# Channel tiles in another order, the key weights' low parts on VectorE, and five small places beside 47 large ones

## The chip, the cores and the metric

The kernel runs on one core of a Trainium2 chip. Its time is the device time of one launch in microseconds (us), as a median of several runs. In the profile PE is TensorE, DVE is VectorE, ACT is ScalarE, POOL is GpSimd, and SP (SyncE) issues all DMAs. Another kernel of this size is told apart from it where the two differ by some 0.2%, that is 2.3 us.

## The reference

One layer of a streaming encoder for 1024 tokens of width 1024, in fp32, with three parts, each between two root-mean-square norms and added to the input:

```python
h = rms_norm(x, pre_mix_g[l])
z = h @ w_in[l] + b_in[l]                       # 1024 -> 1792
y_a = pool_mixer(z_a, ...)                      # trailing-window means, windows 2, 4, 8, 16
y_b = spatial_gating_mixer(z_b, ...)            # gelu, layer norm, 128-position mixing
y_c = conformer_conv_mixer(z_c, ...)            # a * sigmoid(g), causal conv of 31 taps, layer norm, silu
x = x + rms_norm(concat(y_a, y_b, y_c) @ w_out[l], post_mix_g[l])
h = rms_norm(x, pre_x_g[l]); m = rms_norm(mem, mem_g[l])
x = x + rms_norm(memory_cross_attention(h, m, wq[l], wk[l], wv[l], wo[l]), post_x_g[l])
h = rms_norm(x, pre_ff_g[l])
x = x + rms_norm(square(relu(h @ w_ff1[l])) @ w_ff2[l], post_ff_g[l])
```

The memory has 256 tokens, the attention 4 heads of 256, the last part 4096 hidden columns.

## The kernel before

**Arithmetic.** An fp32 factor is split into a high part of type fp32r and a low part (factor minus high part), and a product is three matmuls: high by high, low by high, high by low (`mm3`, L445). The high part is a cast on ACT; the low part is one subtraction on DVE or POOL, called "lo" below (`lo_of`, L438; tile names end in h and l). The large projections (output projection om, queries pq, attention output ox, both parts of the feed-forward part, FF1 and FF2) are done with seven half-size products in place of eight (`seven`, L991).

**Stages.** First x is normed and transposed (p0t, `norm_in`, L558). Then come the channel tiles of the convolution: for j = 0 to 2 (128 channels each) and the two halves hf of the tokens, PE makes zg and za (L602 on); ACT makes sg, the sigmoid of zg; DVE makes hc, the gated channels, and hs, a sum of neighbouring tokens. A convolution of 31 taps over one j needs hc[j] and hs[j] of both halves. It is 47 DVE instructions over rows of 512 (`conv_taps`, L644; accumulators cacca, caccb, caccc). While DVE works on the three j, PE goes on with the gating part (zb, sv, ybt), the pooling part (zaT, pya), the values of the memory (wvp) and the keys of the memory (wkp, from memory tiles mT). Then the convolution's result cs is transposed into token order (cnat), normed over channels (cst, cmv, then cr..e on DVE and cr..r on POOL, a reciprocal square root, then cn on DVE), transposed back (cback), gated on ACT (csg) and put into yq, which the output projection reads (`conv_norm`, L666). The keys are transposed as well (kt, from kn; kT). After that om begins.

**Weights of the first stages.** `row_unit` (L504) loads 128 rows of a weight as 128x1024, casts them on ACT and makes the lo either in one DVE instruction of 128x1024 or in two POOL instructions of 128x512, by the lists ZR, WK and WV (L519). WK are the keys' weights, tiles wk0 to wk7.

**Storage.** All large tiles in on-chip memory lie in NS = 50 places of 4 KB per partition with the tag "s" (`slot`, L113; `put`, L123 gives the recorded tile its place at the end). A tile of 512 floats, such as hs or sg, takes a whole place. The DMA that loads a tile waits until the place's former tile has been read for the last time.

**Order.** The class `Schedule` (L66) records every operation with its dependences, then puts them in order by a list schedule (`_order`, L249) with a cost for each operation (`_cost`, L204), a latency between engines and, for all engines but PE, a due time: that of the PE instruction it serves, or for those that serve none, the end plus SLACK (L82). `order` (L231) does this six times, feeding the order of PE back, and keeps the order with the shortest planned span. A DMA also depends on the PE operation that was recorded 150 before (LEAD). So a number in a cost or a changed number of places moves instructions of every engine, all over the program. On the chip each engine runs its own list in that order, and waits at an instruction whose input isn't there.

Of the kernel before, what the change touches and what calls it, by code (L numbers as in the profile page):

```python
# [20 lines left out]
NK = D // P  # L21
# [5 lines left out]
WINDOWS = (2, 4, 8, 16)  # L27
TAPS = 31
LEAD = 150
NS = 50  # L30


class _Op:
# [32 lines left out]
class Schedule:  # L66
# [12 lines left out]
           "pe": {"act": 197, "dve": 196, "pe": 0, "pool": 200, "sync": 100},  # L79
           "pool": {"act": 75, "dve": 60, "pe": 309, "pool": 102, "sync": 100},  # L80
           "sync": {"act": 2100, "dve": 2100, "pe": 2100, "pool": 2100, "sync": 2100}}
    SLACK = 50000.0  # L82
    PASSES = 6
    BYDUE = ("act", "dve", "pool", "sync")
    TABLE = {AF.Sigmoid: "sigmoid", AF.Gelu_apprx_tanh: "gelu", AF.Exp: "exp"}
# [25 lines left out]
        self.pool, self.places, self.form = pool, n, form  # L111

    def slot(self, name, shape, dt):  # L113
        self._add("s:" + name, "s", self.places)
        self.tiles["s:" + name].update(shape=[128] + list(shape), dt=dt, ap=None)
        n = int(np.prod(shape))
        t = self.form[:, :n]
        if len(shape) > 1:
            d = "abc"[:len(shape)]
            t = t.rearrange(f"p ({' '.join(d)}) -> p {' '.join(d)}", **dict(zip(d, shape)))  # L120
        return _Slot("s:" + name, t if dt == F32 else t.bitcast(dt))

    def put(self, a):  # L123
        if not isinstance(a, _Slot):
            return a
        r = self.tiles[a.name]
        if r["ap"] is None:
            r["ap"] = self.pool.tile(r["shape"], r["dt"], tag=f"s{r['at']}", name=a.name[2:])
        return a.place(r["ap"])


# [71 lines left out]
    @staticmethod  # L203
    def _cost(eng, method, args, kw, ins):  # L204
        n = 1
        for d in args[0].shape[1:]:
            n *= d
        if method == "dma_start":
            return max(450.0, n * args[0].shape[0] * 4 / 240.0)
        size = lambda a: int(np.prod(a.shape[1:]))  # L210
        if eng == "pe":
            passes = 4 if method == "matmul" and args[1].dtype == F32 else 1
            return max(109.0, 13.4 + passes * n * 0.4167)
        wide = [a for a in ins if size(a) > 1]
        ptrs = len(ins) - len(wide) if n > 1 else 0
        if eng == "act":
            c = 51.0 + 0.833 * n + (0.0 if ins[0].space == bass.MemoryType.PSUM else 42.0)
            return c + 93.0 * min(ptrs, 1) + (93.0 if "accum_out" in kw else 0.0)
        if eng == "pool":
            if method == "tensor_tensor":  # L220
                return 520.0 if n < 17 else 60 + 2.4 * n
            return 60 + 1.0 * n
        n = max([n] + [size(a) for a in wide])
        psum = any(a.space == bass.MemoryType.PSUM for a in ins + [args[0]])
        if not psum and len(wide) == 1 and method in ("tensor_scalar", "tensor_scalar_mul",
                                                      "tensor_copy"):
            return 69 + 0.52 * n + 61.0 * ptrs
        return 69 + 1.042 * n + 61.0 * ptrs
# [174 lines left out]
def block_kernel(ctx: ExitStack, tc: tile.TileContext, x, mem, pre_mix_g, w_in, b_in, pool_w,  # L403
# [5 lines left out]
    act, dve, pool, pe, sync = sc.act, sc.dve, sc.pool, sc.pe, sc.sync  # L409
# [106 lines left out]
            return hi, lo  # L516
        return go

    ZR, WK, WV = [pool] * NK, [pool] * NK, [dve] * NK  # L519
    units, made = {}, {}  # L520
    for j in range(3):
        units[f"zc{j}"] = col_unit(f"zc{j}", [(w_in, 1024 + j * P), (w_in, 1408 + j * P)], j == 0)
# [76 lines left out]

    hc = [slot(f"hc{j}", [2, H]) for j in range(3)]  # L600
    hs = [slot(f"hs{j}", [H]) for j in range(3)]
    for j, hf in ((0, 0), (1, 0), (0, 1), (1, 1), (2, 0), (2, 1)):  # L602
        w = W(f"zc{j}")
        pa, pg = bank(f"za{j}{hf}"), bank(f"zg{j}{hf}")
        if (j, hf) == (0, 0):
            for q in range(2):
                if q:
                    norm_in(0, [2, 3])
                prod_t(pg, w, 128, 256, h1[hf], q * 256, q * 256 + 256)
                prod_t(pa, w, 0, 128, h1[hf], q * 256, q * 256 + 256)  # L610
            W("zc1")
            norm_in(1, [0, 1, 2, 3])
            (g_x, g_ff, g_mem, bA, bC, pscale, cb, clg, clb, sgb) = columns("vec", [
                (pre_x_g, 8), (pre_ff_g, 8), (mem_g, 8), (b_in[:, 0:256], 2), (b_in[:, 1024:1792], 6),
                (pool_scale, 2), (conv_b, 3), (conv_ln_g, 3), (conv_ln_b, 3), (sg_b[0], 4)])
            cw = columns("taps", [(conv_w[0].rearrange("k (j p) -> (k j) p", p=P), 93)])[0].rearrange(
                "p (k j) -> p k j", j=3)
        else:
            prod_t(pg, w, 128, 256, h1[hf])
            prod_t(pa, w, 0, 128, h1[hf])  # L620
        sg = slot(f"sg{j}{hf}", [H])
        act.activation(sg, pg, AF.Sigmoid, bias=bC[:, 3 + j:4 + j])
        c = slice(hf * 256, hf * 256 + 256)
        dve.scalar_tensor_tensor(hc[j][:, :, c], pa.rearrange("p (n t) -> p t n", t=2),
                                 bC[:, j:j + 1], sg.rearrange("p (n t) -> p t n", t=2),
                                 ALU.add, ALU.mult)
        dve.tensor_tensor(hs[j][:, c], hc[j][:, 0, c], hc[j][:, 1, c], ALU.add)
# [131 lines left out]
    for hf in range(2):  # L759
        for m in range(2):  # L760
            zaT[hf][m] = slot(f"zaT{hf}{m}", [H + 16])
        for pr in range(2):
# [3 lines left out]
            for i in range(2):  # L766
                b = pr * 2 + i
                p0, p1 = bank(f"zb0{hf}{b}"), bank(f"zb1{hf}{b}")
                for k in range(NK):
                    a = h1[hf][k]  # L770
# [15 lines left out]
                r = rstd_of(f"vr{hf}{b}", mv[:, 1:2], 1)  # L786
# [32 lines left out]
    for t in range(2):  # L819
# [4 lines left out]
        r = rstd_of(f"memr{t}", ms, 1)  # L824
# [475 lines left out]
    for u in range(2, HF // 256):  # L1300
        w, h, rest = ff1(u)
# [29 lines left out]
    for ch in range(2):  # L1331
# [17 lines left out]
        for i, g, first in ((1, 0, True), (2, 1, True), (6, 0, False), (5, 1, True), (7, 0, False),  # L1349
                            (3, 1, False), (4, 0, False)):  # L1350
            ops = []
            for e in range(4):
# [13 lines left out]
                a = slot(f"ha{ch}{i}{e}", [2, H])  # L1366
# [66 lines left out]
```

## Time and profile before

| | |
|---|---|
| time, median of 3 runs | 1169.54 us (1169.51 to 1169.66) |
| the profiled execution's own time | 1169.37 us |
| its span, first to last instruction | 1167.7 us |
| PE busy | 1142.2 us, 98% |
| DVE busy | 917.0 us, 79% |
| ACT busy | 570.9 us, 49% |
| POOL busy | 168.2 us, 14% |
| mean granted TensorE clock | 0.995 |
| DMA | 163.11 MB, 140 GB/s in the mean |

The span leaves 1.7 us of the execution outside. An engine's busy time is summed over its instructions; the granted clock is the part of full speed that the chip gave TensorE. The waits of an engine are listed with the instruction that ended them, and the timeline gives each instruction's start and duration.

### The profile page before, as it was taken

The numbers are of one execution on the slowest core, as the hardware profiler recorded it, in microseconds if no ns is written. First come the engines' busy times: TensorE is split into PE (matmuls) and PEld (weight loads), VectorE is DVE, ScalarE is ACT, GpSimd is POOL, SyncE is SP. The second block draws the span as 40 slices with busy tenths as digits, with TensorE's granted clock in tenths as the row PEclk, the third lists the DMA queues.
The fourth block names the chain that finished last, engine by engine and source line by source line (L and its number), as shares of the span: only waits on it lengthen the run. The fifth ranks groups of instructions, "written<-read, shape, count | busy, mean of one in ns | idle before, by whom it ended". The sixth has DMA issues, their size and how long they took to land.

```text
span 1167.7 us, 14569 instructions
## 1 busy us (share of the span) xinstructions
PE 1142.2 (98%) x5319; PEld 948.6 (81%) x5319; DVE 917.0 (79%) x1278; ACT 570.9 (49%) x998; POOL 168.2 (14%) x194
## 2 busy tenths in 40 slices
PE   7999999799999999999999999999999999999997
PEld 6788877688887898888888888888888888888885
DVE  5499999898988769988999777567679744487736
ACT  6332145666984368749843343334446433435321
POOL 4360229301347000013000000000000000000001
PEclk9999999899999999999999999999999999999999
DMA  7400025114761222236045535443775444443443
GB/s 263 146 30 1 1 89 207 47 62 150 256 253 55 90 72 91 73 119 225 17 136 210 186 137 184 158 146 116 241 263 189 162 163 155 153 160 116 174 144 145
DMA packets 87078, 163.11 MB, mean 140 GB/s; under 512 B 6474, under 2 KB 29918, under 8 KB 87006
## 3 DMA queue, kind: packets, MB, share of 16 engines
q1 hardware_dynamic: 87006, 162.17, 39.8%
q8 instruction: 42, 0.69, 0.2%
q14 instruction: 30, 0.25, 0.1%
HBM read 116.01 MB, written 46.14 MB: 139 GB/s over the span
## 4 chain that ended last, share of the span: by engine, by line
PE 87%; DVE 7%; ACT 4%; issue 1%; POOL 0%; DMA 0%; POOLq 0%; DVEq 0%; ACTq 0%
PE g L162 25%; PE fx L162 13%; PE fz L162 7%; PE om L162 7%; PE pq L162 6%; PE ox L162 5%; PE zb L162 4%; PE fy L162 3%; PE zg L162 3%; PE za L162 3%; PE sc L162 2%; PE o L162 2%; PE wvp L162 2%; PE wkp L162 2%; DVE caccc L162 1%; ACT oxh L162 1%
## 5 line engine op out<-in xcount | busy, mean ns | idle before, releaser
L162 POOL TENSOR_TENSOR fr0r<-fr0e,half 128x1 f32<-128x1 f32 x1 | 0.9, 863 | 581.9 <-DVE fr0e L162 581.9
L162 ACT COPY c<-fx 128x512 f32<-128x512 f32 x48 | 29.0, 603 | 87.8 <-PE fx L162 84.6
L162 DVE TENSOR_TENSOR acc<-acc,g 128x512 f32<-128x512 f32 x40 | 26.9, 684 | 46.1 <-PE g L162 46.1
L162 DVE TENSOR_TENSOR c<-c,fz 128x512 f32<-128x512 f32 x32 | 22.0, 687 | 16.5 <-ACT c L162 16.5
L162 DVE SCALAR_TENSOR_TENSOR c<-c 128x512 f32<-128x512 f32 x48 | 33.3, 693 | 0.7
L162 DVE SCALAR_TENSOR_TENSOR caccc<-hs,cws,caccc 128x511 f32<-128x511 f32 (+14 forms) x45 | 33.5, 744 | 0.2
L162 DVE SCALAR_TENSOR_TENSOR cacca<-hc,taps,cacca 128x511 f32<-128x511 f32 (+14 forms) x45 | 32.2, 746 | 0.0
L162 ACT ACTIVATE junk<-acc 128x512 f32<-128x512 f32 x16 | 10.2, 635 | 44.7 <-DVE acc L162 42.7
L162 DVE TENSOR_TENSOR w1o<-w1a,w1o 128x512 fp32r<-128x512 f32 x32 | 21.6, 689 | 12.6 <-ACT w1o L162 12.6
L162 DVE SCALAR_TENSOR_TENSOR caccb<-hc,taps,caccb 128x511 f32<-128x511 f32 (+13 forms) x42 | 30.5, 745 | 0.0
L162 PE MATMUL sc<-kv,q 128*128 128x256 f32 x192 | 27.5, 288 | 0.0
L162 ACT CAST w1o<-w1a 128x512 fp32r<-128x512 f32 x32 | 19.6, 640 | 14.7 <-DVE sb L162 6.2
L162 PEld LDWEIGHTS sc<-kv,q 128*128 128x128 f32 x192 | 24.9, 190 | 0.7
L162 DVE TENSOR_TENSOR sa<-c 128x512 f32<-128x512 f32 x16 | 11.1, 695 | 18.0 <-ACT c L162 16.5
L162 ACT ACTIVATE c<-fx 128x512 f32<-128x512 f32 x16 | 9.6, 598 | 31.6 <-PE fx L162 31.6
L162 PE MATMUL o<-pT,kv 128*128 128x512 f32 x96 | 24.4, 393 | 0.0
L162 ACT CAST w1o<-w1c 128x512 fp32r<-128x512 f32 x32 | 19.5, 624 | 6.9 <-PE fx L162 4.1
L162 PE MATMUL fx<-h3a10h,w1o 128*128 128x512 f32 x64 | 22.7, 392 | 0.0
L162 DVE TENSOR_TENSOR w1o<-w1c,w1o 128x512 fp32r<-128x512 f32 x32 | 21.6, 689 | 1.2 <-ACT w1o L162 1.2
L162 PE MATMUL fx<-h3a60h,w1o 128*128 128x512 f32 x64 | 22.5, 389 | 0.0
L162 PE MATMUL fx<-h3a11h,w1o 128*128 128x512 f32 x64 | 22.3, 389 | 0.0
L162 PE MATMUL fx<-h3a70h,w1o 128*128 128x512 f32 x64 | 22.3, 389 | 0.0
(1656 smaller groups left out, 4116.8 us busy)
## 6 DMA issues: line engine op xcount, KB each, us to landing
ha<-scr_hid SPq DMA_DIRECT2D x56, 512.0 KB
scr_hid<-c SPq DMA_DIRECT2D x48, 256.0 KB
scr_hid<-sa SPq DMA_DIRECT2D x32, 256.0 KB
scr_hid<-sb SPq DMA_DIRECT2D x32, 256.0 KB
x<-in_x_dram SPq DMA_DIRECT2D x8, 512.0 KB
omwb<-in_w_out_dram SPq DMA_DIRECT2D x8, 512.0 KB
omx<-in_x_dram SPq DMA_DIRECT2D x8, 512.0 KB
scr_x<-omx SPq DMA_DIRECT2D x8, 512.0 KB
```

Source lines behind the costliest of these rows:

```text
L162: op.fn = lambda: f(*[put(a) for a in args], **{k: put(v) for k, v in kw.items()})
```

## The change

The 50 places of 4 KB become 47, and five places of 2 KB with the tag "h" come beside them. Tiles with names that begin with hs or sg and that have at most 528 elements per partition go to the small places: hs0 to hs2, the six sg of the channel tiles, and sgr, the raw mixing matrix. SLACK is 20000 in place of 50000, and the schedule's rate for a DMA 260 in place of 240. The list WK names DVE in place of POOL: eight lo of 128x1024 on DVE in place of sixteen of 128x512 on POOL. The channel tiles come in the order (j, hf) = (0,0), (0,1), (1,0), (1,1), (2,0), (2,1); before, (1,0) stood second.

```diff
--- before.py
+++ after.py
@@ -27,7 +27,10 @@
 WINDOWS = (2, 4, 8, 16)
 TAPS = 31
 LEAD = 150
-NS = 50
+NS = 47
+NH2 = 5
+SMALL = 528
+HALF = ("hs", "sg")
 
 
 class _Op:
@@ -79,7 +82,7 @@
            "pe": {"act": 197, "dve": 196, "pe": 0, "pool": 200, "sync": 100},
            "pool": {"act": 75, "dve": 60, "pe": 309, "pool": 102, "sync": 100},
            "sync": {"act": 2100, "dve": 2100, "pe": 2100, "pool": 2100, "sync": 2100}}
-    SLACK = 50000.0
+    SLACK = 20000.0
     PASSES = 6
     BYDUE = ("act", "dve", "pool", "sync")
     TABLE = {AF.Sigmoid: "sigmoid", AF.Gelu_apprx_tanh: "gelu", AF.Exp: "exp"}
@@ -111,7 +114,10 @@
         self.pool, self.places, self.form = pool, n, form
 
     def slot(self, name, shape, dt):
-        self._add("s:" + name, "s", self.places)
+        if int(np.prod(shape)) <= SMALL and name.startswith(HALF):
+            self._add("s:" + name, "h", NH2)
+        else:
+            self._add("s:" + name, "s", self.places)
         self.tiles["s:" + name].update(shape=[128] + list(shape), dt=dt, ap=None)
         n = int(np.prod(shape))
         t = self.form[:, :n]
@@ -125,7 +131,7 @@
             return a
         r = self.tiles[a.name]
         if r["ap"] is None:
-            r["ap"] = self.pool.tile(r["shape"], r["dt"], tag=f"s{r['at']}", name=a.name[2:])
+            r["ap"] = self.pool.tile(r["shape"], r["dt"], tag=f"{r['tag']}{r['at']}", name=a.name[2:])
         return a.place(r["ap"])
 
 
@@ -206,7 +212,7 @@
         for d in args[0].shape[1:]:
             n *= d
         if method == "dma_start":
-            return max(450.0, n * args[0].shape[0] * 4 / 240.0)
+            return max(450.0, n * args[0].shape[0] * 4 / 260.0)
         size = lambda a: int(np.prod(a.shape[1:]))
         if eng == "pe":
             passes = 4 if method == "matmul" and args[1].dtype == F32 else 1
@@ -516,7 +522,7 @@
             return hi, lo
         return go
 
-    ZR, WK, WV = [pool] * NK, [pool] * NK, [dve] * NK
+    ZR, WK, WV = [pool] * NK, [dve] * NK, [dve] * NK
     units, made = {}, {}
     for j in range(3):
         units[f"zc{j}"] = col_unit(f"zc{j}", [(w_in, 1024 + j * P), (w_in, 1408 + j * P)], j == 0)
@@ -599,7 +605,7 @@
 
     hc = [slot(f"hc{j}", [2, H]) for j in range(3)]
     hs = [slot(f"hs{j}", [H]) for j in range(3)]
-    for j, hf in ((0, 0), (1, 0), (0, 1), (1, 1), (2, 0), (2, 1)):
+    for j, hf in ((0, 0), (0, 1), (1, 0), (1, 1), (2, 0), (2, 1)):
         w = W(f"zc{j}")
         pa, pg = bank(f"za{j}{hf}"), bank(f"zg{j}{hf}")
         if (j, hf) == (0, 0):
```

Four views of how the instructions move follow. On DVE, behind the constants of the convolution, before: the digits behind za and sg are j and hf.

```order
L162 SCALAR_TENSOR_TENSOR hc0_1079<-za00_90,vec_118,sg00_1072 128x2x256
L162 SCALAR_TENSOR_TENSOR hc1_1087<-za10_122,vec_118,sg10_1077 128x2x256
L162 TENSOR_TENSOR hs0_1092<-hc0_1079 128x256
L162 TENSOR_TENSOR hs1_1096<-hc1_1087 128x256
L162 SCALAR_TENSOR_TENSOR hc0_1079<-za01_124,vec_118,sg01_1117 128x2x256
L162 TENSOR_TENSOR hs0_1092<-hc0_1079 128x256
L162 TENSOR_SCALAR cacca0_234<-hc0_1079,taps_120 128x512
L162 TENSOR_SCALAR caccb0_235<-hc0_1079,taps_120 128x512
```

After, at the same place:

```order
L168 SCALAR_TENSOR_TENSOR hc0_1070<-za00_90,vec_118,sg00_1061 128x2x256
L168 TENSOR_TENSOR hs0_1078<-hc0_1070 128x256
L168 SCALAR_TENSOR_TENSOR hc0_1070<-za01_122,vec_118,sg01_1065 128x2x256
L168 TENSOR_TENSOR hs0_1078<-hc0_1070 128x256
L168 TENSOR_SCALAR cacca0_234<-hc0_1070,taps_120 128x512
L168 TENSOR_SCALAR caccb0_235<-hc0_1070,taps_120 128x512
```

The third channel tile was gated ahead of the first tap before (cacca is the first accumulator); now the taps begin behind the second. All six tiles are still made, and the other four stand among the taps.

On POOL, in the stretch in which the lo of the keys' weights were made, before (zw are the window sums of the pooling part, cr00r to cr13r the convolution norm's reciprocal roots for eight token blocks):

```order
L162 TENSOR_TENSOR wk4l<-wk4r,wk4h 128x512
L162 TENSOR_TENSOR zw_2314<-zw_2291 128x521
L162 TENSOR_TENSOR wk5l<-wk5r,wk5h 128x512
L162 TENSOR_TENSOR zw_2351<-zw_2314 128x513
L162 TENSOR_TENSOR wk5l<-wk5r,wk5h 128x512
L162 TENSOR_TENSOR wk6l<-wk6r,wk6h 128x512 x2
L162 TENSOR_TENSOR wk7l<-wk7r,wk7h 128x512 x2
L162 TENSOR_TENSOR cr00r<-cr00e,half 128x1
```

After, from the first zw of the second token half:

```order
L168 TENSOR_TENSOR zw_2207<-zaT_1774 128x527
L168 TENSOR_TENSOR zw_2225<-zw_2207 128x525
L168 TENSOR_TENSOR zw_2241<-zaT_1793 128x527
L168 TENSOR_TENSOR vr13r<-vr13e,half 128x1
L168 TENSOR_TENSOR cr00r<-cr00e,half 128x1
L168 TENSOR_TENSOR zw_2279<-zw_2241 128x525
L168 TENSOR_TENSOR zw_2293<-zw_2279 128x521
L168 TENSOR_TENSOR zw_2311<-zw_2293 128x513
L168 TENSOR_TENSOR cr01r<-cr01e,half 128x1
```

The wk rows are gone from POOL, and cr00r stands ahead of the last three zw.

On DVE, behind the last tap of the third j, after (zz and vv belong to the gating part, oma10l and oma11l are the low parts of om's second product):

```order
L168 TENSOR_TENSOR wk0l<-wk0r,wk0h 128x1024
L168 BN_STATS vst_194<-zz_2091 128x6
L168 TENSOR_TENSOR wk1l<-wk1r,wk1h 128x1024
L168 BN_AGGR vmv_195<-vst_194 128x2
L168 TENSOR_TENSOR oma10l<-yq_1931,oma10h 128x1024
L168 TENSOR_SCALAR vr12e<-vmv_195 128x1
L168 SCALAR_TENSOR_TENSOR zz_2091<-zz_2091,vmv_195,sgn 128x384
L168 TENSOR_TENSOR oma11l<-yq_1649,oma11h 128x1024
L168 SCALAR_TENSOR_TENSOR vv_2154<-zz_2091,vr12r,sgn 128x384
L168 TENSOR_TENSOR wk2l<-wk2r,wk2h 128x1024
L168 TENSOR_TENSOR wk3l<-wk3r,wk3h 128x1024
L168 TENSOR_TENSOR wk4l<-wk4r,wk4h 128x1024
```

The five rows that write wk0l to wk4l are new on DVE; wk5l to wk7l follow some 35 rows later. The row oma11l, which came behind the last omww11l before, stands ahead of them.

On PE, at the end of the keys' products, before:

```order
L162 MATMUL wkp_229<-wk7l,mT_2212 128x512
L162 MATMUL wkp_229<-wk7h,mT_2238 128x512
L162 MATMUL cback_256<-ident,cn_2471 128x128
L162 MATMUL cback_255<-ident,cn_2490 128x128 x2
L162 MATMUL cback_256<-ident,cn_2490 128x128
L162 MATMUL kt_230<-ident,kn_2442 128x128
L162 MATMUL kt_230<-ident,kn_2463 128x128
L162 MATMUL kt_230<-ident,kn_2442 128x128
L162 MATMUL kt_230<-ident,kn_2463 128x128
L162 MATMUL cnat_286<-ident,cs_1549 128x128
L162 MATMUL cnat_286<-ident,cs_1692 128x128
L162 MATMUL cnat_286<-ident,cs_1703 128x128
```

After:

```order
L168 MATMUL wkp_229<-wk7h,mT_2231 128x512
L168 MATMUL wkp_229<-wk7l,mT_2231 128x512
L168 MATMUL wkp_229<-wk7h,mT_2246 128x512
L168 MATMUL kt_230<-ident,kn_2529 128x128
L168 MATMUL kt_231<-ident,kn_2529 128x128
L168 MATMUL kt_232<-ident,kn_2529 128x128
L168 MATMUL kt_233<-ident,kn_2529 128x128
L168 MATMUL kt_230<-ident,kn_2546 128x128
L168 MATMUL kt_230<-ident,kn_2529 128x128
L168 MATMUL kt_230<-ident,kn_2546 128x128
L168 MATMUL kt_231<-ident,kn_2546 128x128
L168 MATMUL kt_231<-ident,kn_2529 128x128
```

Before, the transposes cback, kt and cnat alternate here, each for another block or key column. After, all but the last two groups of cback and all cnat stand further ahead, singly between the wkp products, and kt and om follow on the keys' products.

## Rows read from the trace of the kernel before

**Rows 1.** The head of the page: the span of the execution and, in part 1, the busy time of each engine, its share of the span and its count of instructions.

```profile
span 1167.7 us, 14569 instructions
...
PE 1142.2 (98%) x5319; PEld 948.6 (81%) x5319; DVE 917.0 (79%) x1278; ACT 570.9 (49%) x998; POOL 168.2 (14%) x194
```

**Rows 2.** Busy time by stretch. Columns: the stretch in us, its length, then for PE, PEld, DVE, ACT and POOL the busy us and the count of recorded instructions, then the granted TensorE clock as a part of full speed, the busy share of the DMA engines and what they moved in GB/s.

```profile
0.00:50.00 50.00, 41.29 (x241) 36.12 (x242) 26.53 (x53) 28.44 (x50) 21.00 (x62) 1.00 0.64 207
...
100.00:200.00 100.00, 97.93 (x459) 79.30 (x458) 97.43 (x196) 35.31 (x65) 37.52 (x41) 1.00 0.21 74
200.00:250.00 50.00, 44.08 (x209) 34.81 (x209) 44.15 (x69) 33.44 (x56) 15.86 (x14) 0.93 0.18 64
...
600.00:1100.00 500.00, 500.00 (x2208) 414.15 (x2207) 357.77 (x431) 206.65 (x286) 0.00 (x0) 1.00 0.49 172
1100.00:1168.00 68.00, 59.97 (x265) 49.35 (x263) 37.55 (x60) 12.80 (x28) 7.17 (x8) 0.97 0.42 155
```

**Rows 3.** The waits of PE: the engine and the tile of the waiting matmul, the engine and tile that ended the wait, then total us, times, longest us. All operations are issued from one helper line, so each row says L162.

```profile
PE gmixp L162 <- DMA gmixr<-in_pre_mix_g_dram: 5.7, 1, 5.7
PE cback L162 <- DVE kT L162: 2.4, 1, 2.4
PE p0t L162 <- DVE x L162: 2.3, 3, 1.2
PE kt L162 <- DVE kT L162: 1.5, 1, 1.5
PE memt L162 <- DVE zz L162: 1.1, 1, 1.1
PE pq L162 <- DVE h2a61l L162: 0.9, 1, 0.9
PE cnat L162 <- DVE cr12e L162: 0.6, 1, 0.6
...
PE zb L162 <- ACT zaT L162: 0.6, 1, 0.6
...
PE pya L162 <- DVE zp L162: 0.4, 1, 0.4
PE cback L162 <- DVE cn L162: 0.4, 1, 0.4
PE cback L162 <- ACT csg L162: 0.3, 1, 0.3
PE kt L162 <- ACT kn L162: 0.2, 1, 0.2
```

**Rows 4.** The same columns as rows 2, for three stretches of 5 us.

```profile
220.00:225.00 5.00, 2.49 (x16) 1.57 (x16) 3.56 (x10) 5.00 (x11) 1.27 (x2) 1.00 0.00 2
225.00:230.00 5.00, 2.26 (x9) 1.47 (x9) 4.97 (x10) 4.85 (x9) 1.46 (x1) 0.50 0.00 0
230.00:235.00 5.00, 5.00 (x24) 4.41 (x23) 4.43 (x6) 5.00 (x10) 0.00 (x0) 0.82 0.00 0
```

**Rows 5.** All ScalarE instructions that write csg: count, shortest, median and longest in ns, first and last start in us.

```profile
L162 ACT ACTIVATE csg<-cback,vec x24: 554/588/632, 219.7 to 236.5; 128x256 f32<-128x256 f32 x24
```

**Rows 6.** POOL in time: start us, duration us (of a group in one row, the whole), engine, line, operation, tiles, size, count, and in brackets the idle time before it and what ended that.

```profile
175.31 2.56 POOL L162 TENSOR_TENSOR wk0l<-wk0r,wk0h 128x512 fp32r<-128x512 f32 x2 [8.25 <-ACT wk0h L162]
...
183.67 3.49 POOL L162 TENSOR_TENSOR wk3l<-wk3r,wk3h 128x512 fp32r<-128x512 f32 x2
187.13 1.06 POOL L162 TENSOR_TENSOR zw<-zaT 128x527 f32<-128x527 f32 x1
...
204.23 3.41 POOL L162 TENSOR_TENSOR wk7l<-wk7r,wk7h 128x512 fp32r<-128x512 f32 x2
207.60 0.99 POOL L162 TENSOR_TENSOR cr00r<-cr00e,half 128x1 f32<-128x1 f32 x1
```

**Rows 7.** VectorE in time, the same columns, in the stretch in which POOL does the work of rows 6.

```profile
180.70 3.07 DVE L162 SCALAR_TENSOR_TENSOR caccc<-hs,cws,caccc 128x502 f32<-128x502 f32 x4
183.68 2.35 DVE L162 TENSOR_TENSOR oma10l<-yq,oma10h 128x1024 fp32r<-128x1024 f32 x1
...
193.23 0.15 DVE L162 TENSOR_SCALAR cr00e<-cmv 128x1 f32<-128x1 f32 x1
...
203.29 4.90 DVE L162 SCALAR_TENSOR_TENSOR zp<-zw,zaT 64x512 f32<-64x512 f32 x3
...
213.45 1.22 DVE L162 TENSOR_TENSOR oma11l<-yq,oma11h 128x1024 fp32r<-128x1024 f32 x1
214.58 0.67 DVE L162 TENSOR_SCALAR cn<-cnat,cmv,cr00r 128x384 f32<-128x384 f32 x1
```

**Rows 8.** VectorE in time, from the second to the third channel tile.

```profile
43.93 0.75 DVE L162 SCALAR_TENSOR_TENSOR hc<-za,vec,sg 128x512 f32<-128x512 f32 x1 [4.72 <-PE za L162]
...
54.40 0.75 DVE L162 SCALAR_TENSOR_TENSOR hc<-za,vec,sg 128x512 f32<-128x512 f32 x1 [9.06 <-PE za L162]
...
55.53 0.75 DVE L162 TENSOR_SCALAR cacca<-hc,taps 128x512 f32<-128x512 f32 x1
56.19 0.74 DVE L162 TENSOR_SCALAR caccb<-hc,taps 128x512 f32<-128x512 f32 x1
```

**Rows 9.** One stretch of FF2, columns as rows 2.

```profile
840.00:860.00 20.00, 20.00 (x90) 16.57 (x89) 18.12 (x22) 10.49 (x13) 0.00 (x0) 1.00 0.95 326
```

**Rows 10.** One of the waits of ScalarE, columns as rows 3.

```profile
ACT ho140h L162 <- DMA ha<-scr_hid: 7.1, 1, 7.1
```

## The prediction

> **What bounds the kernel now.** I read the page first for the balance. PE works in 1142.2 of the 1167.7 us of span, so all that a change can win without less PE work lies in the other 25.5 us [rows 1]. The table by stretch says where these are: 8.7 us in the first 50, 2.1 between 100 and 200, 5.9 between 200 and 250, 8.0 behind 1100, and none between 600 and 1100, where FF1 and FF2 keep PE full [rows 2]. The list of PE's waits gives them names [rows 3]. The largest, 5.7 us for the gains' DMA, is the start of the kernel, and the 8.0 us at the end are a tail in which PE has nothing left; the change touches neither. Six rows belong to the hand-over from the memory's keys to the output projection: cback 2.4, 0.4 and 0.3, kt 1.5 and 0.2, cnat 0.6, together 5.4 us. They lie in one place, as the finer table shows: PE works 2.49 and 2.26 of 5 us from 220 to 230, and in the second of these and in part of the third TensorE is granted half its clock, 1.2 in place of 2.4 GHz, right after PE has stood idle about half the time [rows 4].
>
> **Why PE waits there.** cback transposes cn, and cn needs cr00r from POOL. Its input cr00e was there at 193.23 [rows 7], but POOL began cr00r only at 207.60, 14.4 us later, since the lo of the keys' weights, from wk0l at 175.31 to wk7l at 204.23, stood ahead of it in POOL's list [rows 6]. cn followed at 214.58 [rows 7]. So all eight token blocks of the convolution norm came late and at once: the 24 csg on ACT, 588 ns each, 14.1 us of ACT, run only from 219.7 on [rows 5], beside the evacuations of kn and kT that PE waits for too.
>
> **The channel tiles' order.** The first tap stands behind hc and hs of two tiles in either kernel's data, but before it had a third tile ahead of it in DVE's list. DVE gated the second tile at 43.93, then sat idle 9.06 us, and gated the third at 54.40; the first tap began at 55.53 [rows 8]. After, the second tile already completes j = 0. The first tap can begin 54.40 - 43.93 = 10.5 us earlier. The gating of the remaining four tiles is on DVE in both kernels, so it costs nothing more, unless a tap waits behind an hc whose za isn't done: a tile is 10.5 us of PE by the two hc, and taps of j = 0 fill that. I allow 0 to 2 us, inside DVE's lead below.
>
> **WK on DVE.** Added to DVE: eight lo of 128x1024. One such instruction without POOL beside it takes 1.22 us, and the next starts 1.13 us behind it (213.45 to 214.58) [rows 7], so 8 x 1.13 = 9.0 us. Removed from POOL: sixteen of some 1.3 to 1.7 us. Removed with them is what they cost DVE: oma10l, the same shape, took 2.35 us beside wk3l, 1.13 more, and three zp took 4.90 us beside wk6l and wk7l [rows 6, 7]; by oma10l's ratio, 1.22 to 2.35, 2.4 us of that would go. That is 3.5 us from these rows; other DVE instructions beside the sixteen may have lost as much again, 7 at most. I take 5. So DVE comes to the convolution norm 10.5 - 9.0 + 5 = 6.5 us earlier than before (4 to 8.5), and no longer needs POOL for it but for the cr..r themselves, which now stand behind window sums of 1.06 us each [rows 6].
>
> What follows on the path: cn of the first block stands ahead of wk5l in DVE's list after, so cback and csg spread over the last 20 us of the wkp products. The 5.4 us of waits go: all of it if ACT has its 14.1 us of csg and the kn copies behind it in time, which I think likely, because six of the eight groups of cback now stand ahead of the last wkp product in PE's order. What is late next is om itself, which needs the lo of its second and third products from DVE. Being 6.5 us ahead on DVE, with PE ahead by some 8 at that point, is about even, since om's lo's weren't waited for before at all [rows 3]. I charge 1 us for new short waits (0 to 2). With PE not idle, the half clock goes too. From 225 to 230 PE worked 2.26 us at half clock, so 1.1 us lost; from 230 to 235 the mean was 0.82, so up to 0.9 [rows 4]. By clock alone, were PE never without work, it would be 2.5 + 0.9 = 3.4. I take 1.5 (0 to 3.4).
>
> **Other waits of PE.** memt waits 1.1 us for zz [rows 3]. After, zz stands behind five of the new lo's, 5.7 us, and oma11l, 1.1; against it are 10.5 us of the earlier start and 1.1 us of oma10l's stretch. It comes 4.8 us earlier, and 1.1 goes (0 to 1.1). pya's 0.4 us wait for a zp goes with POOL's lo's (0 to 0.4). p0t waits 2.3 us for x in the start [rows 3]; the cast and lo of the second weight unit move behind the second half's norm there, which frees DVE's scale of x of POOL's company: I take 0.8 (0 to 2.3). pq's 0.9 us stands behind another POOL lo that the change doesn't remove but that the new order may shift: 0.4 (0 to 0.9). zb's 0.6 stays.
>
> **Places, SLACK and the DMA rate.** They remove and add no instruction. They act by the order alone; in the first 250 us that is counted above. Behind it the work of PE has no gaps that matter, so an order that keeps PE fed costs nothing, and one that doesn't can only lose. Three large places fewer means that loads in FF1 and FF2 start later. Counted in the order after, the tightest reloads have about 73 matmuls between the last use of a place's former tile and the first use of the new one; at 500/2208 = 0.226 us each [rows 2] that is 16.5 us. A 512 KB load takes 0.524 MB / 326 GB/s = 1.6 us where the DMA engines are dense [rows 9], and the cast and lo behind it some 2.3, at oma11l's 1.22 [rows 7] and about as much on ACT. That fits with a wide margin, so I charge 0 (0 to 14, below).
>
> **Sum.** 5.4 + 1.5 + 1.1 + 0.4 + 0.8 + 0.4 - 1.0 - 0 = 8.6 us. The profiled execution took 1169.37, 0.17 under the median of the runs; 1169.37 - 8.6 + 0.17 is about 1160.9. With every gain at its upper end it would be 5.4 + 3.4 + 1.1 + 0.4 + 2.3 + 0.9 = 13.5, 1156.0; I don't expect more than three quarters of that excess to come together.
>
> **Rivals.** First, that DVE and POOL collide again. POOL's window sums still read memory beside DVE's new lo's. oma10l lost 1.13 us to one POOL neighbour [rows 7]; six window sums of 1.06 us in this stretch could each cost DVE that much, 6.8 us, and DVE's lead would be gone. om's lo's, about even in the forecast, would be late by 6.8 less the slack that they have, which the trace doesn't show; taking half, 3.5 us come back: 1164.4. Against it, four taps beside wk2l and wk3l took 3.07 us, 0.77 each, against a pitch of 0.66 (55.53 to 56.19), so a loss of only 0.1 each [rows 7, 8]. The Trainium skill ("SBUF — State Buffer", section "Who interferes with whom") has it that a DVE instruction with two inputs in SBUF contends with a GpSimd instruction that reads SBUF, whichever starts first blocking the other whole. By that rule each window sum would cost the lo beside it up to its own 1.06 us; That makes the 1164.4 above. oma10l bears it out; the taps, which have two such inputs as well, hardly show it on DVE.
>
> Second, that the wait isn't POOL's: if ACT, with 24 csg, kn and the high parts of kT, is what ends last, the 5.4 us return in another place and the clock with them: 8.6 - 5.4 - 1.5 = 1.7 won, 1167.8. For it speaks that ACT is busy 4.85 to 5.00 of each 5 us from 220 on [rows 4] and that two of the waits name csg and kn [rows 3]; against it that ACT has 35.31 busy us in the 100 before [rows 2].
>
> Third, and this one ends slower: the places. In FF2 the loads of ha come from a store that went out shortly before, and ACT already waited 7.1 us for one of them [rows 10], with no PE wait in FF2 since 16 and more us of reserve stood behind it. Three places less take 3 x 1.6 = 4.8 us of lead away in each dense stretch. It decides if the store or the DMA queue is behind by more than what is left of 16.5 us. Then each of the two halves waits between 4.8 and 7.1 us; at 6, 12 us and the end is 1160.9 + 12 = 1172.9. Against it: the densest stretch moved 326 GB/s [rows 9] 1.6 us a load, and by that rate 16.5 us are ten loads.
>
> **Chances.** The forecast 0.55, DVE and POOL 0.17, ACT 0.12, the places 0.11; 0.05 is left for an order that stalls somewhere I haven't looked. A measurement of this kernel tells 0.2% from no change, 2.3 us, so faster is below 1167.2. Forecast and first rival are faster, and a third of the second: 0.77. Two thirds of the second and some of the third and the rest are the same: 0.11. Slower than 1171.9: 0.12. The range goes from 1157.0, half of the further gains, to 1168.5, which takes in the first two rivals.
>
> **What would show it.** In the profile after: the first tap near 44 to 45 us; no wk on POOL and cr00r within 3 us of cr00e; csg spread from before 200 us; PE idle between 200 and 250 under 2 us with the clock at 1.00 there; no PE wait in 600 to 1100. I am wrong if PE waits for kT, csg or om's lo's by more than 3 us in that stretch, or if any PE wait for an ho or wo tile appears in FF2.

## The result, and the profile after

The changed kernel takes 1157.84 us (median of 4 runs, 1157.65 to 1158.01) beside 1169.6 of the kernel before on the same chip: a ratio of 0.9897, with a 95% interval of 0.9879 to 0.9914. That is 11.8 us faster; 8.6 were forecast, and the range held the time. The head of the page of the profile after:

```profile
span 1156.0 us, 14629 instructions
...
PE 1138.4 (98%) x5319; PEld 946.4 (82%) x5319; DVE 930.8 (81%) x1286; ACT 574.0 (50%) x998; POOL 155.0 (13%) x178
```

The span is 11.7 us shorter [rows 1]. PE's busy time fell by 3.8 us though its matmuls are the same 5319, and its idle time by 7.9. The table by stretch, columns as in rows 2:

```profile
100.00:200.00 100.00, 99.63 (x469) 80.48 (x468) 97.40 (x196) 36.91 (x68) 25.53 (x32) 1.00 0.21 70
200.00:250.00 50.00, 48.82 (x239) 39.52 (x238) 47.13 (x72) 36.31 (x61) 7.31 (x6) 1.00 0.23 82
...
600.00:1100.00 500.00, 500.00 (x2206) 413.79 (x2205) 356.07 (x421) 207.71 (x283) 0.00 (x0) 1.00 0.49 170
```

Between 200 and 250 us PE is now idle 1.2 us in place of 5.9, and the granted clock is 1.00 in place of 0.93; between 100 and 200 it is idle 0.4 in place of 2.1 [rows 2]. FF1 and FF2 are as full as before. PE's waits after, the ones that matter here:

```profile
PE p0t L168 <- DVE x L168: 1.9, 2, 1.4
PE om L168 <- DVE oma60l L168: 0.8, 1, 0.8
...
PE cnat L168 <- ACT csg L168: 0.2, 1, 0.2
...
PE sv L168 <- DVE vv L168: 0.2, 1, 0.2
PE kt L168 <- ACT kn L168: 0.2, 1, 0.2
```

Every cback wait and the waits for kT, cn and zz are gone [rows 3]; new are one of 0.8 us for om's lo oma60l and one of 0.2 in sv. The 5 us stretches of the former trouble [rows 4]:

```profile
220.00:225.00 5.00, 5.00 (x27) 4.14 (x26) 3.82 (x8) 5.00 (x11) 0.00 (x0) 1.00 0.00 0
225.00:230.00 5.00, 5.00 (x23) 4.13 (x22) 5.00 (x8) 2.66 (x6) 0.00 (x0) 1.00 0.01 3
230.00:235.00 5.00, 5.00 (x23) 4.13 (x22) 5.00 (x6) 4.37 (x5) 0.00 (x0) 1.00 0.01 2
```

Half the clock isn't granted anywhere here. POOL around cr00r:

```profile
188.83 0.86 POOL L168 TENSOR_TENSOR cr00r<-cr00e,half 128x1 f32<-128x1 f32 x1
189.66 3.74 POOL L168 TENSOR_TENSOR zw<-zw 128x525 f32<-128x525 f32 x3
```

cr00r begins 0.2 us behind cr00e (188.61, below), where 14.4 us lay between them before [rows 6, 7]. VectorE there:

```profile
182.83 1.23 DVE L168 TENSOR_TENSOR wk4l<-wk4r,wk4h 128x1024 fp32r<-128x1024 f32 x1 [0.38 <-ACT wk4h L168]
...
188.61 0.14 DVE L168 TENSOR_SCALAR cr00e<-cmv 128x1 f32<-128x1 f32 x1
...
189.84 1.29 DVE L168 SCALAR_TENSOR_TENSOR vv<-zz,vr13r,sgn 128x384 f32<-128x384 f32 x1
191.05 0.67 DVE L168 TENSOR_SCALAR cn<-cnat,cmv,cr00r 128x384 f32<-128x384 f32 x1
```

cn comes at 191.05 where it came at 214.58 [rows 7]. A new lo, wk4l, takes 1.23 us, as the forecast had it. vv took 1.29 us beside the window sums that began at 189.66. ACT's csg and the first tap:

```profile
L168 ACT ACTIVATE csg<-cback,vec x24: 555/582/730, 200.8 to 224.3; 128x256 f32<-128x256 f32 x24
```

```profile
42.53 0.75 DVE L168 SCALAR_TENSOR_TENSOR hc<-za,vec,sg 128x512 f32<-128x512 f32 x1 [3.13 <-PE za L168]
...
43.75 0.74 DVE L168 TENSOR_SCALAR cacca<-hc,taps 128x512 f32<-128x512 f32 x1
```

The csg begin at 200.8 in place of 219.7 [rows 5], and the first tap 11.8 us earlier [rows 8]. Read from the timelines, by the start of a stage's first or the last matmul, the gain builds up so:

| up to | before, us | after, us | gained so far | in this part |
|---|---|---|---|---|
| last za (channel tiles) | 86.55 | 85.56 | 0.99 | 0.99 |
| first wkp (keys) | 189.16 | 185.82 | 3.34 | 2.35 |
| last om | 311.31 | 301.18 | 10.13 | 6.79 |
| first sc (attention) | 414.20 | 403.36 | 10.84 | 0.71 |
| end of the span | 1167.7 | 1156.0 | 11.7 | 0.86 |

Two of these parts can be split into PE's idle and busy time. From the first wkp to the last om, before and then after, columns as in rows 2:

```profile
189.16:311.31 122.15, 116.23 (x547) 94.53 (x547) 110.00 (x163) 83.74 (x156) 33.77 (x32) 0.97 0.36 127
185.82:301.18 115.36, 114.03 (x546) 92.90 (x546) 105.17 (x162) 84.96 (x162) 23.21 (x24) 1.00 0.36 129
```

Idle time fell from 5.92 to 1.33 us, 4.6 of the 6.79, and busy time by 2.2, for nearly the same matmuls (547 and 546 are recorded) with the granted clock at 1.00 in place of 0.97. Up to the last za:

```profile
0.00:86.55 86.55, 77.84 (x403) 66.37 (x404) 58.64 (x104) 38.00 (x60) 41.13 (x78) 1.00 0.45 148
0.00:85.56 85.56, 76.89 (x403) 65.69 (x404) 67.42 (x118) 38.69 (x62) 41.06 (x78) 1.00 0.45 150
```

Here the idle time is the same, 8.71 and 8.67 us.

### The profile page after: what moved, and what is told of

The parts are those of the page before. It is cut to its first block, busy times and chain, and to the rows that moved or that the text cites. A ratio compares the mean times of both kernels' runs of the same rounds, so it can differ in the third digit from the quotient of the medians.

```text
span 1156.0 us, 14629 instructions
## 1 busy us (share of the span) xinstructions
PE 1138.4 (98%) x5319; PEld 946.4 (82%) x5319; DVE 930.8 (81%) x1286; ACT 574.0 (50%) x998; POOL 155.0 (13%) x178
## 4 chain that ended last, share of the span: by engine, by line
PE 92%; DVE 3%; ACT 3%; issue 1%; POOL 0%; DMA 0%; POOLq 0%; DVEq 0%; ACTq 0%
PE g L168 25%; PE fx L168 15%; PE zb L168 8%; PE fz L168 8%; PE ox L168 7%; PE pq L168 6%; PE om L168 5%; PE fy L168 4%; PE zg L168 3%; PE za L168 3%; PE sc L168 2%; PE o L168 2%; PE wvp L168 2%; ACT csg L168 1%; PE pT L168 1%
## 5 line engine op out<-in xcount | busy, mean ns | idle before, releaser
L168 PE MATMUL fz<-h3a50h,w1o 128*128 128x512 f32 x64 | 22.5, 389 | 0.0
L168 PE MATMUL fx<-h3a41h,w1o 128*128 128x512 f32 x64 | 22.3, 389 | 0.0
```

The lines of the kernel that those rows point to most:

```text
L168: op.fn = lambda: f(*[put(a) for a in args], **{k: put(v) for k, v in kw.items()})
```

## The experiments

The change has four parts: the tile order, the keys' weights on VectorE, the places, and the two numbers SLACK and DMA rate. Since every edit lets the schedule order the whole program anew, each experiment was chosen by what its order does at the disputed instructions. Ratios are to the kernel before, run on the same chip; the chips' times of it were 1169.97, 1171.29 and 1170.12 us in the three groups of runs.

| kernel | tile order | wk lo's | places | SLACK, rate | ratio (95% interval) |
|---|---|---|---|---|---|
| changed | new | DVE | 47 + 5 | 20000, 260 | 0.9897 (0.9879 to 0.9914) |
| before_wk | old | DVE | 50 | 50000, 240 | 1.0023 (1.0012 to 1.0035) |
| before_order | new | POOL | 50 | 50000, 240 | 1.0016 (1.0007 to 1.0026) |
| before_order_wk | new | DVE | 50 | 50000, 240 | 0.9960 (0.9946 to 0.9974) |
| before_pow_first | old | POOL, roots first | 50 | 50000, 240 | 0.9980 (0.9971 to 0.9990) |
| after_old_slack_rate | new | DVE | 47 + 5 | 50000, 240 | 0.9959 (0.9944 to 0.9974) |
| after_old_places | new | DVE | 50 | 20000, 260 | 0.9929 (0.9915 to 0.9944) |
| after_wk_pool | new | POOL | 47 + 5 | 20000, 260 | 0.9949 (0.9932 to 0.9965) |
| after_wk_pool_pow_first | new | POOL, roots first | 47 + 5 | 20000, 260 | 0.9915 (0.9900 to 0.9930) |
| after_rate_240 | new | DVE | 47 + 5 | 20000, 240 | 0.9918 (0.9901 to 0.9934) |
| after_slack_50000 | new | DVE | 47 + 5 | 50000, 260 | 0.9948 (0.9934 to 0.9963) |
| after_old_order | old | DVE | 47 + 5 | 20000, 260 | 0.9997 (0.9988 to 1.0007) |
| after_pow_first | new | DVE, roots first | 47 + 5 | 20000, 260 | 0.9891 (0.9876 to 0.9906) |

**The tile order alone, on the kernel before.**

```diff
-    for j, hf in ((0, 0), (1, 0), (0, 1), (1, 1), (2, 0), (2, 1)):
+    for j, hf in ((0, 0), (0, 1), (1, 0), (1, 1), (2, 0), (2, 1)):
```

> The kernel before with one edit: the channel tiles in the new order. The taps begin behind the second tile; the wk lo's stay on POOL, and in POOL's list cr00r still stands behind all of them; cback, kt and cnat still stand together at the end of the wkp products. Theory A: the first tap starts near 44 us, DVE comes some 11 us earlier to the norm, and the waits between 215 and 231 us stay within 1 us of the 5.4, with the half clock: 1166 to 1169. Theory B: the 10.5 us on DVE take the waits away: 1158 to 1162.

It is slower, by 0.16%, less than the 0.2% that tells two kernels apart; it is in any case no gain. The first tap comes early, and cr00r doesn't; VectorE, then POOL:

```profile
44.87 0.74 DVE L162 TENSOR_SCALAR cacca<-hc,taps 128x512 f32<-128x512 f32 x1
```

```profile
206.06 3.43 POOL L162 TENSOR_TENSOR wk7l<-wk7r,wk7h 128x512 fp32r<-128x512 f32 x2
209.46 1.53 POOL L162 TENSOR_TENSOR cr00r<-cr00e,half 128x1 f32<-128x1 f32 x1
```

Its input cr00e began at 195.63, so cr00r came 13.8 us behind it, after the wk lo's, and PE is still idle for 4.2 us between 215 and 235, where it was for 5.5 before. Theory B falls: 10.7 us more of VectorE time bought 1.3 us there. Theory A's place is confirmed, though the kernel is even slower than A's range: PE waited 2.2 us in sv for vv, 1.7 of it at 145 us, where eleven taps stand in VectorE's list between vr03e and the first of the two instructions that make this vv (more under "The places").

**The keys' weights alone, on the kernel before.**

```diff
-    ZR, WK, WV = [pool] * NK, [pool] * NK, [dve] * NK
+    ZR, WK, WV = [pool] * NK, [dve] * NK, [dve] * NK
```

> The kernel before with one edit: the keys' weights' lo on DVE. The order that results has no wk on POOL, cr00r behind cr00e at once, and cback standing in six groups among the wkp products; the taps still begin behind the third channel tile. Theory A (cr00r's place in POOL's list made the waits between 215 and 231 us): these waits go even with the old tile order, 5.4 us and the half clock with them, 3 us; DVE is 9 us later for om's lo's less 5 us of stretching, which gives 2 to 4 us of new waits back: 1162 to 1165. Theory B (DVE's late start of the taps made them): DVE has 9 us more to do and starts as late, so the waits stay or grow: 1168 to 1174.

It is the slowest of all that ran, 0.23% over the kernel before, in B's range and not in A's; the profiled execution took 1175.57 us, 2.0 above the median. The cback waits went, as A had it, and om began 4.5 us earlier (226.89 against 231.36), but other waits came, PE's first:

```profile
PE om L162 <- DVE kT L162: 3.1, 1, 3.1
...
PE memt L162 <- ACT zaT L162: 1.6, 1, 1.6
PE om L162 <- DVE oma60l L162: 1.3, 1, 1.3
PE zat L162 <- ACT zaT L162: 1.2, 1, 1.2
```

om ended 6.9 us later than before (318.22 against 311.31). The zat and memt waits stand together, and the granted clock fell behind them, in the second and third of these stretches:

```profile
185.00:190.00 5.00, 2.46 (x19) 1.75 (x17) 4.43 (x10) 3.91 (x9) 2.13 (x2) 0.95 0.45 153
190.00:195.00 5.00, 4.51 (x13) 3.63 (x14) 3.20 (x10) 4.45 (x8) 3.69 (x4) 0.50 0.46 171
195.00:200.00 5.00, 5.00 (x23) 3.98 (x22) 2.52 (x9) 0.00 (x0) 2.32 (x3) 0.87 0.00 0
```

So the waits of cback went as A has it, but A's price for the lateness of VectorE, 2 to 4 us, was far too low, and B named the time.

**Both together, on the kernel before.** The two edits above in one kernel.

> The kernel before with two edits, the tile order and the keys' weights on DVE; 50 places of 4 KB, SLACK and the DMA rate as before. Theory C (these two are the whole gain): within 1.5 us of the changed kernel, 1157 to 1159.5. Theory D (the places, SLACK or the DMA rate carry a good part): over 1161.

0.9960, or 1164.97 us: 5.0 us gained where each alone loses 1.9 to 2.7 (by the ratios). The two need each other, and C falls: 7 us of the change's gain are not in these two.

**POOL's queue alone.** A reciprocal root goes ahead of what else is ready on POOL; every operation stays on its engine.

```diff
             op.due = due[i] if op.eng in self.BYDUE else op.prio
+            if op.eng == "pool" and op.cost == 520.0:
+                op.due = 0.0
```

> The kernel before with one edit in the schedule: a reciprocal root on POOL goes ahead of whatever else is ready there. Work stays on its engines and the tile order is the old one; in the order that results cr00r and cr01r stand between the wk lo's, and cback in seven groups among the wkp products. Theory A: the waits between 215 and 231 us go by this alone; DVE carries no wk lo, but its oma and zp are still stretched: 1160 to 1164. Theory B: it doesn't matter when cr00r comes: 1168 to 1171.

0.9980, or 1167.51 us, 2.5 faster, 3.5 short of A's range and just under B's. The waits of cback and kt for kT and cn are gone by this alone, which is A; in their place PE waits in om:

```profile
PE om L162 <- ACT csg L162: 3.1, 1, 3.1
...
PE om L162 <- DVE oma70l L162: 1.9, 1, 1.9
```

om began 5.9 us earlier (225.46) but ended only 0.8 earlier (310.56). The queue made the waits at 215 to 231. The larger of the new ones ends with a csg of ScalarE, which had no idle time there (the fourth busy time):

```profile
220.00:225.00 5.00, 1.99 (x17) 1.51 (x14) 4.70 (x11) 5.00 (x9) 0.00 (x0) 1.00 0.00 0
```

So the prediction's second rival, ScalarE, holds in this kernel; the 1.9 us for oma70l are VectorE's.

**The queue put back into the changed kernel.** WK on POOL again, the reverse of the edit above.

> The changed kernel with the keys' weights' lo back on POOL. cr00r stands behind all of them in POOL's list and the transposes cback and kt stand together behind the wkp products, as in the kernel before. Theory A (the queue on POOL makes the waits between 215 and 231 us): 5 to 6 us of waits and some 2 to 3 us of half clock come back, while VectorE is 9 us lighter: 1164 to 1168. Theory B (VectorE's late taps made them): under 1160.

0.9949: 6.1 us of the 12 are lost (0.9949 - 0.9897 = 0.0052 of 1170 us), as A had it. cr00r starts at 207.70, 17.4 us behind cr00e, and the stretches after 215 look like those of rows 4:

```profile
215.00:220.00 5.00, 3.63 (x25) 2.46 (x24) 5.00 (x15) 3.64 (x7) 1.10 (x2) 1.00 0.00 2
220.00:225.00 5.00, 2.20 (x11) 1.40 (x11) 5.00 (x7) 4.97 (x10) 1.46 (x1) 0.78 0.00 0
225.00:230.00 5.00, 5.00 (x19) 4.18 (x19) 3.46 (x9) 3.73 (x8) 0.00 (x0) 0.54 0.00 0
```

With the roots first on POOL in addition:

> The same, the keys' weights' lo on POOL, with the rule that a reciprocal root goes ahead of whatever else is ready on POOL. cr00r and cr01r stand in the middle of the wk lo's, cback singly among the wkp products. Theory A: the waits go as in the changed kernel, VectorE is 9 us lighter but its instructions beside POOL are stretched by some 5: 1156.5 to 1160. Theory A' (POOL's lo's, at 2.5 us and more a pair, are themselves too late for the wkp products, which now are reached earlier): waits of wkp or om, 1161 to 1166.

0.9915: 4.0 of the 6.1 us come back though all sixteen lo's stay on POOL. The interval overlaps that of the changed kernel; the rest, 2.1 us, goes with waits in om (omt 1.1, omww70l 0.8, oma60l 0.6) and one for zp (0.9). It doesn't decide between A and A': 1161.17 us lies at the lower end of A', and 0.9915 of 1169.6, 1159.7, in A; waits of om are what A' named.

**The old tile order in the changed kernel.** The reverse of the first edit.

> The changed kernel with the channel tiles in the old order. The first tap begins behind the third tile, 10.5 us later; the wk lo's are on VectorE, 9 us of work, and POOL's lo's don't stretch VectorE any more. VectorE is thus some 5 us behind the kernel before at the norm and 11 behind the changed one. Theory F (VectorE's lead is needed to pay for the lo's): the hand-over to om loses 5 to 8 us against the changed kernel, ratio 0.9940 to 0.9970, with waits for mT, zz or om's lo's. Rival G (the lead isn't needed, POOL's queue alone mattered): 0.9895 to 0.9915.

0.9997: all of the gain is gone, more than theory F allowed. The taps begin at 54.71 us, behind 9.67 us of VectorE's idle time; cr00r starts 2.1 us behind cr00e. om starts at 224.75, 5.8 us later than in the changed kernel, and ends 10.7 later. PE's waits:

```profile
PE om0t L168 <- DVE omt L168: 2.6, 1, 2.6
...
PE memt L168 <- ACT zaT L168: 1.4, 1, 1.4
PE om L168 <- ACT csg L168: 1.1, 1, 1.1
PE om L168 <- DVE oma60l L168: 1.1, 1, 1.1
```

**The places.** With NS = 50 and no small places in the changed kernel, and with SLACK and rate put back under the new places:

> The changed kernel with 50 places of 4 KB and no small ones; SLACK 20000, the rate 260, the tile order and the keys' weights on VectorE as in the changed kernel. vr11e stands behind the cs of j = 1 in VectorE's list. Theory D1: 1163 to 1167, with waits of sv for vv of 1 to 2 us. Theory D2: 1157.5 to 1160.

> The changed kernel with SLACK 50000 and the DMA rate 240 of before. What is still open: before with the tile order and the keys' weights on VectorE alone took 1164.97 us, 7 more than the changed kernel; there PE waited 1.7 us in sv for vv and VectorE 3.1 us in zz for zt, and in VectorE's list the norm's vr11e stood behind the convolution's cs of j = 1. In this kernel vr11e stands well ahead of both late cs again. Theory D1 (the places make that order: with hs and sg in small places 47 large ones are left for the rest, where 50 less up to nine were): 1157.5 to 1160, no wait of sv over 0.5 us. Theory D2 (SLACK and the rate carry it): 1163 to 1166.

The edits are these (in after_old_places with the tag and name rule of `slot` and `put` as before, too):

```diff
-NS = 47
-NH2 = 5
+NS = 50
```

```diff
-    SLACK = 20000.0
+    SLACK = 50000.0
...
-            return max(450.0, n * args[0].shape[0] * 4 / 260.0)
+            return max(450.0, n * args[0].shape[0] * 4 / 240.0)
```

0.9929 and 0.9959. The places alone add nothing to the two edits above (0.9959 against 0.9960), and without them the change loses 3.7 us. Both D1 and D2 are half right. In all three kernels with 50 places and the new tile order, PE waits 1.7 us in sv, then 0.7 and 0.5 in ybt. In after_old_places, POOL, VectorE and PE:

```profile
136.59 0.55 POOL L162 TENSOR_TENSOR vr03r<-vr03e,half 128x1 f32<-128x1 f32 x1 [0.20 <-DVE vr03e L162]
```

```profile
144.77 0.61 DVE L162 SCALAR_TENSOR_TENSOR vv<-zz,vr03r,sgn 128x384 f32<-128x384 f32 x1
```

```profile
145.44 1.57 PE L162 MATMUL sv<-vv,swt 128*128 128x192 f32 x8 [1.70 <-DVE vv L162]
```

and the same vv in the changed kernel:

```profile
140.35 0.61 DVE L168 SCALAR_TENSOR_TENSOR vv<-zz,vr03r,sgn 128x384 f32<-128x384 f32 x1
```

The root vr03r is ready by 137.3 us in both kernels. In after_old_places eleven taps stand between vr03e and the first of the two instructions that make the vv, in the changed kernel four. The mark that the expectations go by, vr11e behind cs of j = 1, is there too, but at 160 to 168 us, where PE doesn't wait in sv. A further 1.1 us wait in after_old_places is pq's for wqw61l. The sv and ybt waits are gone in the profile of after_old_slack_rate, where instead om waits 4.0 us for omww70l and loses clock behind it. So the places free the sv, and what they free is lost again in om while SLACK is 50000.

**SLACK and the rate apart.** Each is put back by itself; for SLACK:

```diff
-    SLACK = 20000.0
+    SLACK = 50000.0
```

> The changed kernel with SLACK 50000 alone put back. Theory E1: ratio 0.9935 to 0.9955, start as in the changed kernel, an om wait of some 4 us at the seventh product. Theory E2: 0.9895 to 0.9915.

> The changed kernel with the DMA rate 240 alone put back. With SLACK put back as well the ratio to before was 0.9959, where the changed kernel had 0.9897; its start ran 1.3 us later and om's last products waited 4.0 us for omww70l with half the clock behind it. In this kernel the scale of x by p02r stands one row later in VectorE's list again. Theory E1 (the rate gives the start, SLACK gives om): ratio 0.9900 to 0.9920, the 1.3 us at the start lost and no om wait over 1.5 us. Theory E2 (the rate gives both): 0.9945 to 0.9965.

0.9948 for SLACK put back, 0.9918 for the rate. E1 holds for both, though the rate's interval overlaps that of the changed kernel: the rate gives the start (the last za at 86.56 in place of 85.56 us, and between 85.38 and 85.90 in all kernels with 260, at 86.45 or later in all with 240; the rest of its loss lies in waits of 0.5 to 0.9 us in kt, pq and once in FF2), SLACK gives om, though not by the wait that E1 named. It is om0t, the transpose of the residual's first token block, for omt (omx is a block's sum with its input, omt that sum normed):

```profile
279.34 1.36 PE L168 MATMUL om0t<-ident,omt 128*128 128x128 f32 x8 [2.60 <-DVE omt L168]
```

The clock falls behind it, as the two stretches from 275 on show; PE also waits 0.9 us in pq and 0.6 in the feed-forward part:

```profile
275.00:280.00 5.00, 2.40 (x14) 1.78 (x13) 4.27 (x12) 3.99 (x9) 3.63 (x4) 1.00 0.92 274
280.00:285.00 5.00, 5.00 (x26) 4.22 (x25) 5.00 (x7) 4.46 (x15) 0.92 (x1) 0.66 0.90 331
```

VectorE's list shows why. The lo omww70l of om's seventh product, with SLACK 50000:

```profile
277.27 1.28 DVE L168 SCALAR_TENSOR_TENSOR omx<-omt,oma2r,omx 128x1024 f32<-128x1024 f32 x1
...
278.54 0.75 DVE L168 TENSOR_SCALAR omt<-omx,omb0r 128x1024 f32<-128x1024 f32 x1
...
280.56 1.22 DVE L168 TENSOR_TENSOR omww70l<-omwb,omww70h 128x1024 fp32r<-128x1024 f32 x1
```

and in the changed kernel:

```profile
265.65 1.22 DVE L168 TENSOR_TENSOR omww70l<-omwb,omww70h 128x1024 fp32r<-128x1024 f32 x1
```

With 20000 the lo stands ahead of every omx. With 50000 the omx of three blocks and the first block's omt stand ahead of it, and that omt stands behind the second and third omx (278.54, where it came at 274.68 in the changed kernel). PE's list, made with the same due times, has only four matmuls of the seventh product ahead of om0t then, and PE reaches it at 276.74, before its input is there.

**Roots first in the changed kernel.** The two lines of before_pow_first once more.

> The changed kernel with the rule that a reciprocal root goes ahead of whatever else is ready on POOL. Nothing else on POOL is long there any more. If POOL's queue is spent as a cause: ratio 0.9885 to 0.9910, the order's other chance moves included. If it still holds cn back: 0.9870 to 0.9885, with less waits of cnat and om.

0.9891 against 0.9897: the intervals cover each other, so the queue on POOL is spent as a cause. Its profiled span, 1155.2 us, is the shortest of all, but it can't be told from the changed kernel.

## Why the prediction was right, and where its terms were off

**cr00r's place in POOL's list** was read rightly, from one row of POOL beside one of VectorE [rows 6, 7]. It is shown four ways: taken away alone (before_pow_first), left in place with all else changed (after_wk_pool), and twice with the taps' start moved and the queue kept or removed (before_order, after_old_order).

**The taps' start** gave 11.8 us where 10.5 were forecast, and **the eight lo's** cost 1.21 to 1.23 us each. The prediction joined the two into one lead of VectorE of 6.5 us (cr00e came 4.6 us earlier, 188.61 against 193.23, with five of the eight lo's done) and took that lead as comfort ("about even", 1 us of new waits, and 1.4 measured in om, cnat, kt and sv). after_old_order shows that it is no comfort but a condition: without it nothing is left of the gain. One sign was missed by little: the csg were to spread from before 200 us, and the first came at 200.8.

**The sum.** From the first wkp to the last om the forecast was 5.4 + 1.5 + 0.4 - 1.0 = 6.3 us, and 6.79 were measured. Waits of 5.4 and 0.4 went and 1.4 came; the remaining 2.4 us are what the half clock had cost, by difference (2.2 by PE's busy time in that stretch), where I took 1.5 and gave 3.4 as the bound. The term that was most mis-sized is the part before the keys: 1.1 us forecast for memt, with "zb's 0.6 stays", and 2.35 measured. zb's wait for zaT went too, as did both waits of memt; the zz that memt had waited for began 2.6 us earlier (183.97 against 186.60), where 4.8 were forecast. The start gave 0.99 (0.8 forecast), but by luck: p0t's wait for x fell by 0.4 only, PE's idle time up to the last za is the same in sum, and the gain goes with the DMA rate; how it shortens PE's busy time there isn't shown. The queries gave 0.71 (0.4), and the end 0.86, for which I had nothing.

**"Places, SLACK and the DMA rate ... act by the order alone"** was right, and so was the cost of nothing in FF2: PE is busy for all of 600 to 1100 us. But the step failed in taking them for bystanders of the first 250 us. Without them the two edits that I worked out by rows give 0.9960, 5 us; with them there come the other 7. What they do without the two edits was not run. I had compared the orders of before and after, seen the sum of all edits, and put the whole of it down to the two that move the taps and the wk lo's. The time came out near, 3.2 us off, in part by luck: the forecast was made on the order of the changed kernel as a whole, whose rows carry the places' and SLACK's work without naming it. It wouldn't have been near for the two edits alone.

**The rivals.** DVE and POOL didn't collide beside the new lo's, since the window sums stand behind wk4l and ahead of wk5l. One instruction did lose: vv with 1.29 us beside the window sums, against 0.62 for the one at 179.56. The Trainium skill ("SBUF — State Buffer", "Who interferes with whom") has such an instruction, with two inputs in SBUF, contend with a GpSimd instruction that reads SBUF; this row agrees. The taps that the prediction sets against it are no test: their accumulators cacca to caccc are tiles of `bank`, in PSUM, where the kernel's matmuls put their results, so such a tap has one input in SBUF, where the places are, and not two. ACT wasn't what ended last in the changed kernel (csg ends 0.2 us of PE's waits), though it was with POOL's queue alone mended, and the places' rival in FF2 met no wait.

## What to carry to other kernels

Where one engine's list holds short instructions that a chain needs and long ones that have time, look for the short ones' inputs on the other engines: 14 us between cr00e and cr00r were visible in two rows, and a rule of two lines in the schedule wins 2.5 us in the kernel before and 4.0 in after_wk_pool. Two edits can each lose and together gain when one moves the work that the other makes room for; try them together before either is given up, and in a kernel that a scheduler orders, ask of each number in the scheduler what it moves, by putting it back alone. And a wait of PE costs more than its length where the clock falls behind it, so cost waits with the granted clock of the stretches after them.

## What the runs showed that was not expected

The clock fell to half behind a single wait of 2.6 us (after_slack_50000, with 2.40 of 5 us busy: 0.66 in the next 5 us), and behind 2.8 us of waits in zat and memt (before_wk, 2.46 of 5 busy: 0.50 and 0.87). It didn't fall behind the 1.7, 0.7 and 0.5 us of sv and ybt in after_old_places, where the granted clock of 100 to 200 us stayed 1.00 with PE idle for 3.1; in before_order the same waits leave PE busy for less than half of a stretch, and the clock stays at 1.00:

```profile
145.00:150.00 5.00, 2.13 (x11) 1.63 (x12) 5.00 (x14) 0.37 (x1) 0.43 (x2) 1.00 0.00 0
```

And it fell behind far less in before_order_wk, where p0t, tapsp and zg wait 0.6, 0.4 and 0.4 us in the start. The stretch there, then the same one in the changed kernel, where tapsp and zg wait as long:

```profile
30.00:35.00 5.00, 4.23 (x16) 2.94 (x15) 5.00 (x10) 5.00 (x9) 1.07 (x1) 0.74 0.59 208
```

```profile
30.00:35.00 5.00, 4.24 (x18) 3.32 (x19) 5.00 (x10) 5.00 (x8) 2.17 (x2) 1.00 0.93 369
```

So neither the length of a wait nor the idle time in a place tells by itself, in these rows, if the clock falls. Where it did, the waits cost more than their length.
